# Weight sums for the FFN moved to later steps, a gate split cut in two, and combination factors moved to GpSimd

## The chip, the cores and the metric

The kernel runs on one core of a Trainium2 chip. The metric is the device time of one execution in microseconds (us). A core has five engines that run side by side, each in its own program order: TensorE (PE, matrix products; its weight loads show as PEld), VectorE (DVE), ScalarE (ACT), GpSimd (POOL) and SyncE (SP), which here only issues DMA transfers. Engines wait for one another through semaphores. SBUF is the memory that the engines work in, PSUM the one that PE writes into.

## The reference

One transformer layer on 1024 tokens of width 1024, in float32:

```
h    = rms_norm(x, g1) * (1 + sc1) + sh1
proj = h @ w_in                     # qa ka va | qb kb vb | gates
o_a  = neighbourhood_attention(qa, ka, va, rpb)       # 8 heads
o_g, lse_g = dilated_window_attention(qb, kb, vb, g)  # 3 groups of 4 heads
wts  = softmax(stack(lse_g), axis=0)                  # over the 3 groups
o_b  = sum_g wts[g] * o_g
gate_a, gate_b = sigmoid(gates + b_gate)
x    = x + gt1 * ((gate_a * (o_a @ w_a) + gate_b * (o_b @ w_b)) @ w_o)
h2   = rms_norm(x, g2) * (1 + sc2) + sh2
a, up = split(h2 @ w_ffn_in)                          # FFN
x    = x + gt2 * ((silu(a) * up) @ w_ffn_out)
```

`wts`, the weights over the three dilated groups, are the combination factors of this case.

## The kernel before

Every large product is made of float32 pieces that PE takes at a faster rate: a float32 tile of weights is split into a high part `whi` (ACT, L129 or L1204) and the rest `wlo`, the difference (GpSimd or DVE, L132 or L1210), and the product is the sum of three passes, whi by hi, wlo by hi and whi by lo. A second layer of economy forms products of 2 x 2 blocks from fewer block products, for which sums and differences of weight blocks are needed beforehand. For the gates these are made by `gate_prep`: the blocks w11 and w12 are only split, and x1 and x4 come from sums (L868, L870, L875) that are then split (L132). For the first two column sets of the FFN they are made by `w1_combos`: four loads of 256 KB (L953, tile `w1m`), four sums of 128 by 512 on GpSimd (L957, L959, L961, L963) and four stores (L965) into a scratch tensor in device memory, which the FFN reads back at the far end of the kernel, from 867 us of the trace on.

The middle of the kernel is one loop over steps n = 6 to 91. A step holds some chunks of projection products (from the stream of input projections up to step 75, L1248; from step 76 the gate products, L880), and around them the attention pieces of one or two heads: score products (L579), maximum and bias and exponentials (DVE L593, ACT L594 and L597, the reciprocals L596), turns of probabilities and of queries and keys through PE (L605 and L477), and their copies back (DVE L609, L505, L506; ACT L503, L504, L611). `qk` is the tile of turned queries and keys that the score products read; its high part is written by ACT and by DVE L505, its rest by ACT L504 and DVE L506. DVE also evicts the products (L397, L446, L1168 to L1171) and normalizes queries and keys (L406, L415, L416, L426). L505, L506, L397, L446 and L593 read a PSUM operand; L415, L416 and L426 read two operands that both lie in SBUF.

PE's order is written out by hand and is the same row for row in both kernels. On the other engines and on the SP queue a list scheduler places the instructions, by priorities that follow the order in which the code issues them and by its own costs, except that those under `pin` keep their place among one another. So where the code issues something decides what comes ahead of what on DVE, ACT, GpSimd and SP. Waits are set by data: an instruction that stands ready behind one that waits has to wait too.

Three tables and a function say at which step the pieces here are issued. `GPREP` (L31) maps a step to a pair of gate columns and a part of `gate_prep`: part -2 loads w11 and w12 of a pair, 0 splits them, -1 loads the other two blocks, and 1 makes x1 and x4. `GLOAD` (L32) loads later pairs whole (tile `gl`, two transfers of 1 MB, L841). `W1MIX` (L33) gives the first of the five steps over which each of the two calls of `w1_combos` is spread (L1368). `combine_stats` (L728) works out the combination factors in five parts in steps 68 to 72 from the loaded statistics `sa`, on arrays of 128 by 32: minimum (L738, L739), differences (L742), exponentials (ACT, L743), sum of weighted terms (L745 to L750), reciprocal (L751) and final factors (L754). The factors `fe` are read from step 80 on.

In the trace, steps 68 to 75 lie at about 420 to 485 us, 80 to 91 at about 503 to 588 us.

Of the kernel before, what the change touches and what calls it, by code (L numbers as in the profile page):

```python
# [27 lines left out]
MORD = (3, 4, 5, 6, 7, 2, 0, 1)  # L28
GPAIRS, GGROUPS = ((5, 6), (7, 2), (0, 1), (3, 4)), ((3, 4, 5), (6, 7, 2), (0, 1))
GPHASE = ("w11", "w12", "x1", "x4")  # L30
GPREP = {72: (0, -2), 73: (0, 0), 74: (0, -1), 76: (0, 1), 82: (1, 0), 84: (1, 1), 86: (2, 0), 88: (2, 1), 90: (3, 0)}  # L31
GLOAD = {81: 1, 85: 2, 89: 3}  # L32
W1MIX = (69, 74)  # L33
MC11 = {0: (5, 6, 7, 2), 1: (0, 1)}
MKEEP = {3: 3, 4: 4, 5: 5, 6: 6, 7: 7}
MSLOT = {4: 2, 5: 0, 6: 1}
# [12 lines left out]
def hybrid_layer(ctx: ExitStack, tc: tile.TileContext, x, colp, wada1, wada2, bada2, wqkv, wg, wpa, wpb,  # L49
                 wo, w1, w2, hgain, ropeg, rope, rbias, bmask, g2r, out):  # L50
    nc = tc.nc
# [676 lines left out]
    def combine_stats(part):  # L728
        nm = [cb["sa"][:, :, g, :, 0:2] for g in range(3)]
        sm = [cb["sa"][:, :, g, :, 2:4] for g in range(3)]  # L730
        if part == 0:
            cb["nM"] = ap_.tile([128, 8, 2, 2], F32, tag="nM", bufs=1, name="nM")
            cb["fe"] = ap_.tile([128, 3, 8, 2, 2], F32, tag="fe", bufs=1, name="fe")
            cb["tw"] = ap_.tile([128, 8, 2, 2], F32, tag="tw", bufs=1, name="tw")
            cb["tot"] = ap_.tile([128, 8, 2, 2], F32, tag="tot", bufs=1, name="tot")
        nM, fe, tw, tot = (cb[z] for z in ("nM", "fe", "tw", "tot"))
        if part == 0:
            nc.vector.tensor_tensor(nM, nm[0], nm[1], op=ALU.min)  # L738
            nc.vector.tensor_tensor(nM, nM, nm[2], op=ALU.min)  # L739
        elif part == 1:  # L740
            for g in range(3):
                nc.vector.tensor_sub(fe[:, g], nM, nm[g])  # L742
            nc.scalar.activation(fe, fe, AF.Exp)  # L743
        elif part == 2:
            nc.vector.tensor_mul(tot, fe[:, 0], sm[0])  # L745
            nc.vector.tensor_mul(tw, fe[:, 1], sm[1])
            nc.vector.tensor_add(tot, tot, tw)
        elif part == 3:
            nc.vector.tensor_mul(tw, fe[:, 2], sm[2])
            nc.vector.tensor_add(tot, tot, tw)  # L750
            nc.vector.reciprocal(tot, tot)  # L751
        else:
            for g in range(3):
                nc.vector.tensor_mul(fe[:, g], fe[:, g], tot)  # L754

    def combine_prep(i):
        pr, g, hf = i // 6, (i % 6) // 2, i % 2
# [87 lines left out]
    def gate_prep(p, part):  # L845
        pr = GPAIRS[p]
        if part == -2:
            for i in pr:
                for q in (0, 1):
                    graw[i, q] = gate_raw(i, q)  # L850
            return
        if part == 0:
            for nm, q in (("w11", 0), ("w12", 1)):
                for i in pr:
                    gwt[i, nm] = wsplit(graw[i, q])
            return
        if part == -1:
            z = big("wgx")
            for i in pr:
                for q in (2, 3):  # L860
                    graw[i, q] = gate_raw(i, q) if i == pr[0] else z[:, 512 * q - 1024:512 * q - 512]
            for q in (2, 3):
                pin(nc.sync.dma_start(graw[pr[1], q], wg[pr[1], :, 4 * q:4 * q + 4, :]))
            return
        eng = nc.vector if p == 3 else nc.gpsimd
        for i in pr:
            r = [graw.pop((i, q)) for q in range(4)]
            eng.tensor_add(r[2], r[2], r[3])  # L868
            gwt[i, "x1"] = wsplit(r[2])
            eng.tensor_sub(r[2], r[2], r[0])  # L870
            if p < 3:
                nc.sync.dma_start(sig_d[i, 4], r[2])
            else:
                glate[i] = r[2], r[3]
            eng.tensor_sub(r[1], r[1], r[2])  # L875
            gwt[i, "x4"] = wsplit(r[1], eng)
# [1159 lines left out]
```

## Time and profile before

| | us |
|---|---|
| runs shown | 1478.35, 1470.94, 1472.72 |
| median of these | 1472.72 |
| profiled execution | 1472.6 |
| its span (first to last instruction) | 1470.8 |
| PE busy in the span | 1449.9 |
| DVE busy | 1102.8 |
| GpSimd busy | 732.5 |
| ACT busy | 703.9 |

The profiled execution's own time is 1.8 us above its span, and 0.1 us under the median of the runs. Engine times are the sum of their busy stretches; several engines are busy at once, so they add up to more than the span. The mean granted TensorE clock is 0.998 of full speed: it stands at 1.00 nearly throughout. In a timeline, a row gives the start, the time, the engine, the line, the operation, what is written from what, and in brackets the idle time before it and what ended it.

### The profile page before, as it was taken

To read this page: it belongs to the slowest core of one execution; us is meant where nothing else is said; L and a number is where in the kernel's file an instruction comes from. 1 tells how busy PE (TensorE), PEld (TensorE's weight loads), DVE (VectorE), ACT (ScalarE), POOL (GpSimd) and SP (SyncE) were. 2 spreads that over 40 slices of the span, in tenths; PEclk is the share of its full clock that TensorE was granted. 3 is DMA by queue.
4 is the path that set the end of the run, shared out by engine and by line. 5 is a ranking of instruction groups with operands and counts; after the bars stand their busy time and mean duration, and the time that the engine had idled before them with its cause. 6 is when DMAs were issued, how large, how long until landed. Compare 5 with 4: busy or idle time off the path is not lost.

```text
span 1470.8 us, 24489 instructions
## 1 busy us (share of the span) xinstructions
PE 1449.9 (99%) x8024; PEld 1235.4 (84%) x8024; DVE 1102.8 (75%) x2120; ACT 703.9 (48%) x1771; POOL 732.5 (50%) x706
## 2 busy tenths in 40 slices
PE   8999999999999999999999999999999999999998
PEld 7999999999888777888878888888888888888886
DVE  6688867858688765795877696888777777599578
ACT  5566665666777764554432453332232223354442
POOL 0353466655544455355522303777677775104464
PEclk9999999999999999999999999999999999999999
DMA  9658686766758676955374334445433334898353
GB/s 359 221 169 261 186 266 194 231 198 211 231 176 264 220 243 209 367 191 173 122 257 146 100 101 164 132 148 179 164 100 106 105 107 151 287 348 302 109 157 101
DMA packets 191568, 285.18 MB, mean 194 GB/s; under 512 B 29744, under 2 KB 91856, under 8 KB 190672
## 3 DMA queue, kind: packets, MB, share of 16 engines
q1 hardware_dynamic: 172864, 269.96, 55.4%
q10 hardware_dynamic: 18576, 13.64, 2.8%
q8 instruction: 64, 1.05, 0.3%
q14 instruction: 64, 0.52, 0.1%
HBM read 218.67 MB, written 64.86 MB: 193 GB/s over the span
## 4 chain that ended last, share of the span: by engine, by line
PE 48%; DVE 3%; ACT 1%; DMA 1%; issue 0%; POOL 0%; SPq 0%; ACTq 0%; DVEq 0%
PE ps_s L1695 8%; PE ps_d L1695 7%; PE ps_v L1695 7%; PE ps_t L1695 6%; PE ps_s L1871 4%; PE ps_d L1871 4%; PE ps_t L1871 3%; PE ps_v L1871 3%; PE ps_s L1630 2%; PE ps_d L1630 2%; PE ps_v L1630 1%; DVE sg L1485 1%; DVE wlo L132 1%; DMA sg<-sig_d 1%; ACT h2T L1486 1%; DVE sg L1484 0%
## 5 line engine op out<-in xcount | busy, mean ns | idle before, releaser
L129 ACT ACTIVATE whi<-raw 128x512 fp32r<-128x512 f32 (+2 forms) x265 | 158.3, 608 | 180.0 <-PE ps_s L1871 34.9
L132 POOL TENSOR_TENSOR wlo<-raw,whi 128x512 fp32r<-128x512 f32 (+2 forms) x94 | 128.5, 1375 | 117.3 <-ACT whi L129 114.3
L132 DVE TENSOR_TENSOR wlo<-raw,whi 128x512 fp32r<-128x512 f32 (+1 forms) x171 | 148.9, 888 | 50.1 <-ACT whi L129 47.0
L379 PE MATMUL ps_d<-whi,hT 128*128 128x384 f32 x384 | 101.3, 338 | 0.0
L1645 POOL TENSOR_TENSOR e<-e,c 128x512 f32<-128x512 f32 x44 | 68.8, 1565 | 60.9 <-DVE c L1775 36.8
L129 ACT ACTIVATE whi<-ws 128x512 fp32r<-128x512 f32 x60 | 37.6, 627 | 118.6 <-DVE ws L1712 80.9
L1248 PE MATMUL ps_d<-whi,hT 128*128 128x384 f32 x312 | 88.1, 342 | 1.3 <-DVE hT L1169 1.1
L880 PE MATMUL ps_d<-hT,whi 128*128 128x512 f32 x264 | 84.2, 400 | 0.0
L132 POOL TENSOR_TENSOR wlo<-m,whi 128x512 fp32r<-128x512 f32 x35 | 51.0, 1463 | 51.5 <-ACT whi L129 51.5
L1643 ACT ACTIVATE e<-e 128x512 f32<-128x512 f32 x44 | 27.5, 630 | 98.4 <-DVE e L1778 69.7
L379 PEld LDWEIGHTS ps_d<-whi,hT 128*128 128x128 f32 x384 | 69.6, 188 | 0.6 <-issue 0.6
L1248 PE MATMUL ps_d<-whi,smix 128*128 128x384 f32 x240 | 68.1, 343 | 0.9 <-DMA smix<-t_d 0.6
L1210 POOL TENSOR_TENSOR wlo<-raw,whi 128x384 fp32r<-128x384 f32 x48 | 49.8, 1054 | 30.6 <-ACT whi L1204 30.5
L379 PE MATMUL ps_d<-wlo,hT 128*128 128x384 f32 x192 | 64.2, 334 | 0.0
L658 ACT ACTIVATE P<-P,st 128x256 f32<-128x256 f32 (+2 forms) x100 | 45.6, 458 | 36.2 <-DVE st L656 36.2
L1210 POOL TENSOR_TENSOR wlo<-chain,whi 128x384 fp32r<-128x384 f32 x36 | 37.5, 1055 | 51.0 <-ACT whi L1204 51.0
L1695 PE MATMUL ps_v<-h2T,whi 128*128 128x512 f32 x192 | 59.2, 389 | 0.0
L1695 PE MATMUL ps_s<-h2T,whi 128*128 128x512 f32 x192 | 59.1, 389 | 0.0
L1248 PEld LDWEIGHTS ps_d<-whi,hT 128*128 128x128 f32 x312 | 57.0, 188 | 2.4 <-DVE hT L1169 1.4
L132 POOL TENSOR_TENSOR wlo<-gl,whi 128x512 fp32r<-128x512 f32 x30 | 41.1, 1384 | 32.4 <-ACT whi L129 32.2
L1644 DVE TENSOR_TENSOR e<-e 128x512 f32<-128x512 f32 x44 | 43.6, 999 | 17.7 <-ACT e L1643 17.4
L1695 PE MATMUL ps_d<-h2T,whi 128*128 128x512 f32 x184 | 56.7, 390 | 0.0
(485 smaller groups left out, 4647.8 us busy)
## 6 DMA issues: line engine op xcount, KB each, us to landing
raw<-in_w_dram SPq DMA_DIRECT2D x139, 256.0 KB, 3.3
raw<-in_wqkv_dram SPq DMA_DIRECT2D x116, 192.0 KB, 3.7
ga_d<-e SPq DMA_DIRECT2D x77, 256.0 KB, 2.3
raw<-ga_d SPq DMA_DIRECT2D x77, 256.0 KB, 2.6
smix<-t_d SPq DMA_DIRECT2D x72, 256.0 KB, 4.0
m<-in_w_dram SPq DMA_DIRECT2D x44, 256.0 KB, 5.3
xt<-in_x_dram SPq DMA_DIRECT2D x16, 512.0 KB, 6.4
land<-in_wada_dram SPq DMA_DIRECT2D x16, 512.0 KB, 9.5
```

What stands on the lines that cost most here:

```text
L129: h = nc.scalar.activation(hi[:, :n], r, AF.Copy)
L132: (eng or nc.gpsimd).tensor_sub(lo[:, :n], r, fview(hi[:, :n]))
L379: nc.tensor.matmul(pd[:, :384], tok(a, k, t), U.w[k][b][:, :384], start=(k == 0 and i == 0), stop=(k == KT - 1 and i == 2))
L658: nc.scalar.activation(C.P[h][:nq, c], C.P[h][:nq, c], AF.Exp, scale=-1.0, bias=nm, accum_out=sm)
L880: nc.tensor.matmul(pb, w[x][:, k * 128:(k + 1) * 128], b[y][k], start=(k == 0 and q == 0), stop=(k == 3 and q == 2))
L1210: nc.gpsimd.tensor_sub(lo[:, :384], z, fview(hi[:, :384]))
L1248: nc.tensor.matmul(pd[:, :384], lhs, w[k][b][:, :384], start=(k == 0 and i == 0), stop=(k == 3 and i == 2))
L1630: nc.tensor.matmul(pbs[hf], h2T[a][:, k, t * 128:(t + 1) * 128], wow[hf, k][b], start=(n == 0 and (a, b) == PASS[0]), stop=(n == KT - 1 an ...
L1644: nc.vector.tensor_mul(sg, sg, a)
L1645: nc.gpsimd.tensor_mul(sg, sg, up)
L1695: nc.tensor.matmul(pb, w[p][:, k * 128:(k + 1) * 128], b[q][:, k], start=(k == 0 and i == 0), stop=(k == 3 and i == 2))
L1871: nc.tensor.matmul(pb[m], o[0][a][:, m * 128:(m + 1) * 128], o[1][b], start=(k == 0 and i == 0), stop=(k == HT - 1 and i == 2))
```

## The change

`W1MIX` moves the two sets of FFN weight sums from steps 69 to 73 and 74 to 78 to steps 80 to 84 and 85 to 89. `GPREP` splits w11 of both columns of the first pair in step 73 (part 5) and w12 in step 75 (part 6), instead of both in step 73. In `combine_stats` the eleven differences, products and sums go from DVE to GpSimd; the two minima and the reciprocal stay on DVE, the exponential on ACT.

```diff
@@ -28,9 +28,9 @@
 MORD = (3, 4, 5, 6, 7, 2, 0, 1)
 GPAIRS, GGROUPS = ((5, 6), (7, 2), (0, 1), (3, 4)), ((3, 4, 5), (6, 7, 2), (0, 1))
 GPHASE = ("w11", "w12", "x1", "x4")
-GPREP = {72: (0, -2), 73: (0, 0), 74: (0, -1), 76: (0, 1), 82: (1, 0), 84: (1, 1), 86: (2, 0), 88: (2, 1), 90: (3, 0)}
+GPREP = {72: (0, -2), 73: (0, 5), 74: (0, -1), 75: (0, 6), 76: (0, 1), 82: (1, 0), 84: (1, 1), 86: (2, 0), 88: (2, 1), 90: (3, 0)}
 GLOAD = {81: 1, 85: 2, 89: 3}
-W1MIX = (69, 74)
+W1MIX = (80, 85)
 MC11 = {0: (5, 6, 7, 2), 1: (0, 1)}
 MKEEP = {3: 3, 4: 4, 5: 5, 6: 6, 7: 7}
 MSLOT = {4: 2, 5: 0, 6: 1}
@@ -739,19 +739,19 @@
             nc.vector.tensor_tensor(nM, nM, nm[2], op=ALU.min)
         elif part == 1:
             for g in range(3):
-                nc.vector.tensor_sub(fe[:, g], nM, nm[g])
+                nc.gpsimd.tensor_sub(fe[:, g], nM, nm[g])
             nc.scalar.activation(fe, fe, AF.Exp)
         elif part == 2:
-            nc.vector.tensor_mul(tot, fe[:, 0], sm[0])
-            nc.vector.tensor_mul(tw, fe[:, 1], sm[1])
-            nc.vector.tensor_add(tot, tot, tw)
+            nc.gpsimd.tensor_mul(tot, fe[:, 0], sm[0])
+            nc.gpsimd.tensor_mul(tw, fe[:, 1], sm[1])
+            nc.gpsimd.tensor_add(tot, tot, tw)
         elif part == 3:
-            nc.vector.tensor_mul(tw, fe[:, 2], sm[2])
-            nc.vector.tensor_add(tot, tot, tw)
+            nc.gpsimd.tensor_mul(tw, fe[:, 2], sm[2])
+            nc.gpsimd.tensor_add(tot, tot, tw)
             nc.vector.reciprocal(tot, tot)
         else:
             for g in range(3):
-                nc.vector.tensor_mul(fe[:, g], fe[:, g], tot)
+                nc.gpsimd.tensor_mul(fe[:, g], fe[:, g], tot)
 
     def combine_prep(i):
         pr, g, hf = i // 6, (i % 6) // 2, i % 2
@@ -849,8 +849,8 @@
                 for q in (0, 1):
                     graw[i, q] = gate_raw(i, q)
             return
-        if part == 0:
-            for nm, q in (("w11", 0), ("w12", 1)):
+        if part in (0, 5, 6):
+            for nm, q in (("w11", 0), ("w12", 1))[part // 6:2 - part % 6 // 5]:
                 for i in pr:
                     gwt[i, nm] = wsplit(graw[i, q])
             return
```

With the scheduler placing DVE, ACT, GpSimd and SP, the tables move more than they name. DVE in steps 71 and 72, before: `qk` is the turned-query tile, `qn` the normalized queries and keys, `rz` their factors.

```order
L446 TENSOR_TENSOR hT<-hT,ps_d 128x128
L415 SCALAR_TENSOR_TENSOR rz<-ss_7312,ry 128x8
L416 SCALAR_TENSOR_TENSOR rz<-rz,rv 128x8
L505 SCALAR_TENSOR_TENSOR qk<-ps_v,hg,qk 128x2x64
L426 SCALAR_TENSOR_TENSOR qn<-qn,rz 128x256 x2
L506 TENSOR_TENSOR qk<-ps_v,qk 128x2x64
L397 TENSOR_TENSOR qn<-hT,ps_d 128x256
L446 TENSOR_TENSOR hT<-hT,ps_d 128x128
L406 TENSOR_REDUCE ss_7482<-sq 128x4
L593 ISA P,sx<-ps_s,rb 128x256
L593 ISA sx 128x1
```

The same place on DVE in the changed kernel:

```order
L397 TENSOR_TENSOR qn<-hT,ps_d 128x256
L446 TENSOR_TENSOR hT<-hT,ps_d 128x128
L505 SCALAR_TENSOR_TENSOR qk<-ps_v,hg,qk 128x2x64
L506 TENSOR_TENSOR qk<-ps_v,qk 128x2x64
L397 TENSOR_TENSOR qn<-hT,ps_d 128x256
L415 SCALAR_TENSOR_TENSOR rz<-ss_7304,ry 128x8
L446 TENSOR_TENSOR hT<-hT,ps_d 128x128
L416 SCALAR_TENSOR_TENSOR rz<-rz,rv 128x8
L426 SCALAR_TENSOR_TENSOR qn<-qn,rz 128x256 x2
L406 TENSOR_REDUCE ss_7473<-sq 128x4
L593 ISA P,sx<-ps_s,rb 128x256
```

Before, the two L426 stand between L505 and L506; now L505 and L506 follow each other and stand ahead of L415, L416 and L426.

GpSimd in steps 70 to 76, before (-) and now (+): the splits of `raw` 128x384 are the stream's, the four of 128x512 are those of w11 and w12, and `w1m` are the FFN weight sums.

```order
-L957 TENSOR_TENSOR w1m<-w1m 128x512
-L1210 TENSOR_TENSOR wlo<-raw,whi 128x384 x2
-L959 TENSOR_TENSOR w1m<-w1m 128x512
-L1210 TENSOR_TENSOR wlo<-raw,whi 128x384 x2
-L961 TENSOR_TENSOR w1m<-w1m 128x512
-L963 TENSOR_TENSOR w1m<-w1m 128x512
+L1210 TENSOR_TENSOR wlo<-raw,whi 128x384 x4
 L132 TENSOR_TENSOR wlo<-raw,whi 128x512 x4
-L957 TENSOR_TENSOR w1m<-w1m 128x512
-L959 TENSOR_TENSOR w1m<-w1m 128x512
 L868 TENSOR_TENSOR raw<-raw 128x512
 L868 TENSOR_TENSOR wgx<-wgx 128x512
```

The six sums that lay there are gone; the four splits still follow one another without anything between them, and the first sums of x1 (L868) stand directly behind them.

GpSimd in steps 80 to 86, where the first L957 now stands just ahead of this piece: `gl` are the whole columns of the second pair of gates.

```order
+L959 TENSOR_TENSOR w1m<-w1m 128x512
+L868 TENSOR_TENSOR gl<-gl 128x512
+L132 TENSOR_TENSOR wlo<-gl,whi 128x512
+L868 TENSOR_TENSOR gl<-gl 128x512
+L132 TENSOR_TENSOR wlo<-gl,whi 128x512 x3
 L961 TENSOR_TENSOR w1m<-w1m 128x512
+L132 TENSOR_TENSOR wlo<-gl,whi 128x512
 L963 TENSOR_TENSOR w1m<-w1m 128x512
-L868 TENSOR_TENSOR gl<-gl 128x512
-L132 TENSOR_TENSOR wlo<-gl,whi 128x512
-L868 TENSOR_TENSOR gl<-gl 128x512
-L132 TENSOR_TENSOR wlo<-gl,whi 128x512 x4
```

Two sums stand ahead of the pair's first L868, and two among its splits. On the SP queue, the first set's loads (L953) moved to a place ahead of the first two `gl` loads (L841), the second set's loads ahead of the next two and its stores (L965) ahead of the last two; the loads of the first pair's other two blocks (L120 and L863), which stood behind four stores and four loads of `w1m`, now stand without them. On GpSimd the factors stand among the stream's splits and sums L1199 of steps 68 to 70.

## Rows read from the trace of the kernel before

**Rows 1.** Page, part 1: engine, busy us, share of the span, instructions.
```profile
PE 1449.9 (99%) x8024; PEld 1235.4 (84%) x8024; DVE 1102.8 (75%) x2120; ACT 703.9 (48%) x1771; POOL 732.5 (50%) x706
```

**Rows 2.** Waits of the PE, whole span: line, waited for, total us, times, longest.
```profile
PE ps_s L579 <- DVE qk L506: 3.0, 1, 3.0
...
PE ps_d L1248 <- DVE hT L1169: 1.1, 1, 1.1
...
PE ps_v L477 <- DVE sx L596: 0.6, 1, 0.6
```

**Rows 3.** Windows: us, busy PE, PEld, DVE, ACT, POOL, PEclk, DMA share, GB/s.
```profile
420.00:440.00 20.00, 18.95 (x137) 16.62 (x136) 17.46 (x58) 15.05 (x47) 9.03 (x9) 1.00 0.49 148
467.50:470.60 3.10, 0.09 (x2) 0.00 (x0) 3.10 (x6) 1.49 (x4) 2.16 (x2) 1.00 1.07 393
470.60:474.00 3.40, 3.38 (x22) 2.83 (x23) 2.01 (x8) 2.02 (x8) 0.00 (x0) 0.50 1.03 341
510.00:514.00 4.00, 4.00 (x24) 3.27 (x24) 2.12 (x6) 3.19 (x11) 0.00 (x0) 1.00 0.62 194
514.00:520.00 6.00, 6.00 (x46) 4.48 (x46) 4.22 (x12) 2.96 (x9) 1.26 (x2) 1.00 0.97 360
```

**Rows 4.** Timeline of DVE, 463 to 475: start, us, line, operation, [idle before].
```profile
463.12 0.41 DVE L593 CUSTOM_DVE_ANT_0 P<-ps_s,rb 128x256 f32<-128x256 f32 x1
...
467.26 1.20 DVE L416 SCALAR_TENSOR_TENSOR rz<-rz,rv 128x8 f32<-128x8 f32 x1
468.38 0.42 DVE L505 SCALAR_TENSOR_TENSOR qk<-ps_v,hg,qk 128x128 fp32r<-128x128 f32 x1
468.72 1.56 DVE L426 SCALAR_TENSOR_TENSOR qn<-qn,rz 128x256 f32<-128x256 f32 x2
470.20 0.36 DVE L506 TENSOR_TENSOR qk<-ps_v,qk 128x128 fp32r<-128x128 f32 x1
```

**Rows 5.** Timeline of ACT, 465 to 475.
```profile
466.62 0.43 ACT L504 ACTIVATE qk<-ps_v 128x128 fp32r<-128x128 f32 x1
```

**Rows 6.** Timeline of PE, 454 to 486.
```profile
461.06 0.62 PE L579 MATMUL ps_s<-qk 64*128 64x256 f32 x6
...
467.20 0.38 PE L579 MATMUL ps_s<-qk 64*128 64x256 f32 x2
470.62 0.80 PE L579 MATMUL ps_s<-qk 64*128 64x256 f32 x4 [3.03 <-DVE qk L506]
```

**Rows 7.** Timeline of GpSimd (POOL), 444 to 500.
```profile
465.91 3.75 POOL L132 TENSOR_TENSOR wlo<-raw,whi 128x512 fp32r<-128x512 f32 x3 [0.47 <-ACT whi L129]
...
478.20 1.28 POOL L868 TENSOR_TENSOR raw<-raw 128x512 f32<-128x512 f32 x1
```

**Rows 8.** Timeline of SP's queue, 459 to 480.
```profile
467.92 3.16 SPq L953 DMA_DIRECT2D w1m<-in_w_dram  x4
471.44 1.16 SPq L120 DMA_DIRECT2D raw<-in_wg_dram  x2
```

**Rows 9.** Timeline of DVE, 474 to 486.
```profile
478.69 2.52 DVE L426 SCALAR_TENSOR_TENSOR qn<-qn,rz 128x256 f32<-128x256 f32 x2
```

**Rows 10.** Timeline of DVE, 418 to 432.
```profile
424.89 1.04 DVE L746 TENSOR_TENSOR tw<-fe,sa 128x32 f32<-128x32 f32 x1
```

**Rows 11.** Groups of GpSimd by line, 100 to 300: busy us, mean ns.
```profile
L434 POOL TENSOR_TENSOR rb<-qn,rtab 128x32 f32<-128x32 f32 x35 | 12.2, 348 | 0.0
```

**Rows 12.** Timeline of GpSimd, 498 to 560.
```profile
518.74 1.29 POOL L868 TENSOR_TENSOR gl<-gl 128x512 f32<-128x512 f32 x1 [19.71 <-DMA gl<-in_wg_dram]
519.99 1.32 POOL L132 TENSOR_TENSOR wlo<-gl,whi 128x512 fp32r<-128x512 f32 x1
...
547.31 1.29 POOL L132 TENSOR_TENSOR wlo<-gl,whi 128x512 fp32r<-128x512 f32 x1
```

**Rows 13.** Timeline of PE, 518 to 530.
```profile
523.37 0.40 PE L880 MATMUL ps_d<-hT,wlo 128*128 128x512 f32 x1
```

**Rows 14.** Timeline of PE, 554 to 560.
```profile
556.35 0.40 PE L880 MATMUL ps_d<-hT,wlo 128*128 128x512 f32 x1
```

## The prediction

> **What bounds the kernel now.** I read the engines' busy times first: PE is busy 99% of the span, the next engine, DVE, 75% [rows 1]. So time can only come from PE: from its waits, from its clock, or from new waits put on it. The list of PE's waits, read next, puts a single one on top: score products L579 wait 3.0 us for DVE L506, the last writer of the turned queries and keys; below it, among the waits between 400 and 500 us, are 1.1 us for L1169 and 0.6 us for L596 [rows 2]. The windows then show what the long one costs beyond itself: in 467.5 to 470.6 PE is busy 0.09 of 3.10 us, and in the 3.40 us behind it the granted clock is 0.50, the lower of its two levels (1.2 instead of 2.4 GHz), while PE is busy 3.38 us [rows 3]. At full clock that work takes 1.7 us, so the dip costs 1.7 and stall and dip together 4.7 us.
>
> Last, the timelines around the stall, which tell why L506 is late. ACT's part of the same tile is there at 467.05 (466.62 + 0.43) [rows 5], and PE reaches its first row of L579 at 467.20 [rows 6]. But on DVE, L505 starts at 468.38 behind an L416 that took 1.20 us for 128 by 8 elements, and the two L426, 1.56 us together, stand between L505 and L506 [rows 4]. In the same stretch GpSimd runs three of the first gate's four low-part splits without a break, 465.91 to 469.66, 1.25 us each [rows 7]: L416 ends at 468.46, where the second of them ends (468.41). At 478.69, where GpSimd runs an L868 [rows 7], two L426 take 2.52 us [rows 9]. So operations of DVE that read two SBUF operands get in only where a GpSimd instruction ends, while L505 and L506, which read PSUM, run in 0.42 and 0.36 us in the midst of the splits. The Trainium skill, "SBUF — State Buffer", section on who interferes with whom, has the same: a DVE instruction with two SBUF inputs and a GpSimd one that reads SBUF exclude each other for a whole instruction, one with at most one SBUF input is free; the trace agrees (1.20 us against 0.36 to 0.42).
>
> **The change part by part.** All sums are on the profiled execution: 1472.6 us, 1.8 above its span and 0.1 below the median shown.
>
> *The stall at 467 us.* The stall goes by order, not by a faster engine. In the changed DVE order L505 and L506 follow each other ahead of L415, L416 and L426. ACT's part ends at 467.05, L505 and L506 take 0.42 and 0.36 [rows 4, 5], so L506 ends by about 467.7, and PE, at its first L579 rows until 467.58 [rows 6], waits 0.1 us or nothing: −3.0. The clock fell in this stretch only right behind the stall; with the stall I take away the dip: −1.7. Bounds: 0, if something else on DVE holds L505 as long, and −4.7.
>
> *The two-step gate split.* The four low-part splits still stand back to back on GpSimd, and their loads and ACT's high parts are issued where they were. I give this part 0 by itself (0 to −0.4, L506's remaining lateness).
>
> *What is late next.* Two things follow the splits more closely now. The loads of the first pair's other blocks went out at 471.44, behind the second set's L953 at 467.92 [rows 8] and four stores; without these they go out at 467.9 at the latest, and earlier by the stores' time, right behind the step's own loads. And the two L957 and L959 that stood ahead of L868 are gone. So x1's sums, which began at 478.20 [rows 7], can begin where the splits end, 469.66, and GpSimd works without gaps from 465.9 to about 472.2 (five instructions of 1.25). DVE's L415, L416 and two L426, from 467.9 on, then get in one at each end of a GpSimd instruction: 468.4, 469.7, 470.9, 472.2. Queued behind them on DVE is L593, which begins the softmax of the scores just made. Undisturbed it comes 2.06 us behind the first L579 (463.12 against 461.06) [rows 4, 6], here at 469.3; held, at 472.2. For the probabilities' turn the next step leaves about 2 us of that. The same early sums meet the short last step of the stream, where the chain has no slack already: PE waits 0.6 us for L596 there [rows 2]. Bounds: 0, if the held operations fit into the step, and +4.7, another stall like the first with its dip. Nearest is the 0.6 us wait, twice, with a little from the longer hold: I take +1.4.
>
> *Combination factors.* Eleven instructions of 128 by 32 leave DVE in the stretch 420 to 440, where it is busy 17.46 of 20 us [rows 3]; one of them is L746, held for 1.04 us [rows 10]. Ahead of L1169, for which PE waits 1.1 us, stand only the three L742. Bounds: 0 and −1.1; I take −0.4, for those three and the smaller hold of what follows. On GpSimd the nearest operation of that shape, L434, takes 348 ns [rows 11]: 11 × 0.35 = 3.8 us, laid into 10.97 us of idle time (9.03 of 20 busy) [rows 3]. The last three wait for DVE's reciprocal, and the stream's splits are queued behind them on GpSimd; the factors are read only from step 80 on. If the cover were gone, 3.8 us of GpSimd would delay splits, and PE with them: that is in the upper end.
>
> *Weight sums in steps 80 to 89.* Eight sums of 1.3 us, eight loads and eight stores, 2 MB in and 2 MB out, all moved. Their result is read from 867 us on, so only what they delay counts. First set: L957 and L959 fit into the 19.71 us in which GpSimd sat idle until `gl` landed [rows 12]. Their 1 MB of loads stands ahead of the `gl` loads on the SP queue: at 360 GB/s, the rate when nothing else limits [rows 3], 2.9 us. In the stretch where they can go out, 510 to 514, a DMA share of 0.62 leaves 0.38 × 4 = 1.5 us of room [rows 3], so `gl` lands about 1.4 us later. The first low part from it ends at 521.31 and PE wants it at 523.37 [rows 12, 13]: 2.06 us of slack. That hides it; but ACT, which makes the high parts of `gl` in its own order between softmax pieces, may pass some of it on. I take +0.3 (0 to +2.9). Second set: two sums of the first set among the splits free `gl`'s buffer 2.6 us later, and 1 MB of loads adds 2.9: 5.5 us, against 556.35 − 548.60 = 7.75 us of slack in the next pair [rows 12, 14]. At 0, with +4.7 (a stall with its dip) if the cover is gone; the last pair has a similar distance.
>
> Sum: −3.0 −1.7 +1.4 −0.4 +0.3 = −3.4, so 1472.6 − 3.4 = 1469.2 us.
>
> **The rivals.**
> *B, the wait moves on by a step.* x1's sums hold L415, L416 and L426 as worked out above, L593 comes at 472.2, and PE, instead of waiting for `qk` at 467, waits about 3 us for the probabilities at about 472 or in the short step, and the clock falls again. For it: the two L426 of 2.52 us at 478.69 beside only two L868. Against it: the normalized queries that L426 makes are not needed until steps later, and only the order on DVE passes the hold on. The sum has +4.7 in place of +1.4: 1472.5 us. The rule of the Trainium skill ("SBUF — State Buffer", who interferes with whom) that the second one blocks in full for the whole instruction speaks for this end.
>
> *C, slower: `gl` comes late.* The weight sums push each of the three later pairs' `gl` past the slack: decided by whether the first low part slips by more than 2.06 us (second pair) and 7.75 us (third), where I reckon 1.4 and 5.5. Each pair then costs a stall with a dip, 4.7 us: 1472.6 − 3.0 − 1.7 − 0.4 + 14.1 + 1.4 = 1483.0. For it: the DMA share is 0.97 in 514 to 520 already [rows 3], so anything added there is late in full. Against it: both slacks.
>
> *D, the change does not do what it says.* Splitting in two steps leaves the splits together, and DVE is still held by them ahead of L505: the order ahead of it has the evictions L397 and L446 alone, but if L505 slips behind a wait of those, stall and dip stay: 1472.6 − 0.4 + 0.3 = 1472.5.
>
> **How the numbers follow.** My forecast 0.60, with 1466.2 to 1471.5 as its own range: the low end is 1472.6 less all that rows 2 and 3 offer between 400 and 500 us, 3.0 + 1.7 + 1.1 + 0.6 = 6.4. B 0.20 (1471.5 to 1474), D 0.08, C 0.12, of which a third with a single late pair (1473 to 1476) and two thirds with two or three. Half a per cent, about what a measurement of this kernel can tell, is 7.4 us: faster means below 1465.4, slower above 1480.1. Faster then needs more than the waits that I can name, by a shift of the runs against the profiled execution or by a wait elsewhere: 0.09. Slower is most of C: 0.08. The rest, 0.83, is within. The range, 1465.5 to 1476.5, takes in the forecast, B and D and a single late pair.
>
> **What would show it.** Right: no wait of L579 for L506 near 467 us, L505 and L506 next to each other, and a granted clock of 1.00 throughout 460 to 480; L868 starting near 470; some wait of 0.5 to 1.5 us of L605 or L477 for ACT or DVE in 470 to 485; no factor on DVE and less than 1.1 us at L1169; `gl` landing 1 to 2 us later with no wait of L880. Wrong: a wait over 2 us with a clock of 0.50 behind it anywhere in 420 to 590. If it stands in 470 to 485 it is B, at 467 D, at L880 or behind a low part of `gl` C.

## The result and the profile after

| | us |
|---|---|
| before, median of 6 runs | 1472.22 |
| after, median of 6 runs | 1484.41 (1483.52 to 1484.92) |
| ratio after / before | 1.0083, 95% interval 1.0071 to 1.0096 |
| profiled execution, and its span | 1484.92, 1483.1 |

The change made the kernel 0.83% slower; the predicted 1469.2 us and the range up to 1476.5 both miss it. PE has the same instructions in the same order in both kernels, so the time can be followed matmul by matmul: the start of one in the trace of after, less its start in the trace of before.

| stretch in before, us | shift at its start and end, us | lost (+) or gained (−) |
|---|---|---|
| 0 to 460 | 0, −1.7 | −1.7 |
| 460 to 475, the stall at 467 | −1.7, −6.6 | −4.9 |
| 475 to 490 | −6.6, −3.3 | +3.3 |
| 490 to 545 | −3.3, −2.9 | +0.4 |
| 545 to 562, third pair of gates | −2.9, 4.6 | +7.5 |
| 650 to 690 | 4.6, 7.1 | +2.5 |
| 735 to 765, the merge of the gates | 7.1, 12.5 | +5.4 |
| 765 to the end | 12.5, 12.3 | −0.2 |

The first row is not the change's: it arises at about 30 us, long before any edited instruction, and every kernel below shows something like it (0.4 to 2.7 us less at 100 us), though the code there is the same.

The page of after, part 1, against [rows 1]: PE's busy time grew by 5.7 us of the 12.3, by work at the lower clock; the rest is waits.

```profile
PE 1455.6 (98%) x8024; PEld 1237.9 (83%) x8024; DVE 1096.1 (74%) x2109; ACT 703.9 (47%) x1771; POOL 733.3 (49%) x717
```

The waits of PE in after between 380 and 800 us (line, waited for, total, times, longest). L506 of [rows 2] is gone; of the two on top the first is new, and the second has grown: before, it read `PE ps_d L1630 <- DVE sg L1484: 1.3, 1, 1.3`.

```profile
PE ps_d L880 <- ACT P L597: 4.9, 1, 4.9
PE ps_d L1630 <- DVE sg L1484: 4.0, 1, 4.0
PE ps_v L620 <- DVE PT L609: 1.5, 1, 1.5
PE ps_s L880 <- DVE wlo L132: 1.1, 1, 1.1
PE ps_t L352 <- DVE acc L367: 1.0, 1, 1.0
...
PE ps_d L1248 <- DVE hT L1169: 0.6, 1, 0.6
```

The windows of after (us, busy PE, PEld, DVE, ACT, POOL, clock, DMA share, GB/s). Behind each of the three new waits the clock is low. What that costs is the busy time by the missing share of the clock: 4.38 × 0.34 = 1.5, 5.05 × 0.45 = 2.3 and 5.00 × 0.50 = 2.5 us. With the waits, 1.5, 4.9 and 4.0 − 1.3, this makes 3.0, 7.2 and 5.2 us, against the shifts of 3.3, 7.5 and 5.4.

```profile
460.00:477.00 17.00, 15.50 (x119) 12.99 (x117) 13.71 (x43) 12.62 (x43) 11.73 (x9) 1.00 0.57 184
...
477.00:482.00 5.00, 4.38 (x20) 3.61 (x21) 3.85 (x15) 4.97 (x16) 3.58 (x3) 0.66 0.09 26
...
555.80:563.00 7.20, 5.05 (x12) 3.80 (x12) 4.25 (x7) 2.59 (x8) 7.20 (x7) 0.55 0.37 125
...
752.00:757.00 5.00, 5.00 (x12) 3.93 (x13) 4.12 (x5) 1.79 (x4) 2.53 (x2) 0.50 0.82 246
```

**467 us: the stall is gone.** DVE in after, 463 to 478, the answer to [rows 4] and [rows 9]:

```profile
463.88 0.45 DVE L505 SCALAR_TENSOR_TENSOR qk<-ps_v,hg,qk 128x128 fp32r<-128x128 f32 x1 [0.84 <-ACT qk L504]
464.24 0.40 DVE L506 TENSOR_TENSOR qk<-ps_v,qk 128x128 fp32r<-128x128 f32 x1
...
465.51 1.12 DVE L416 SCALAR_TENSOR_TENSOR rz<-rz,rv 128x8 f32<-128x8 f32 x1
466.66 0.76 DVE L426 SCALAR_TENSOR_TENSOR qn<-qn,rz 128x256 f32<-128x256 f32 x2
...
473.74 0.98 DVE L416 SCALAR_TENSOR_TENSOR rz<-rz,rv 128x8 f32<-128x8 f32 x1
474.75 1.83 DVE L426 SCALAR_TENSOR_TENSOR qn<-qn,rz 128x256 f32<-128x256 f32 x2
...
476.57 0.40 DVE L609 COPY PT<-ps_t 128x256 f32<-128x256 f32 x1
```

L506 ends at 464.64, and the score products L579 begin without a wait at 465.44. L416 still takes 1.12 us beside GpSimd's splits, but it now stands behind L506. The clock is 1.00 in 460 to 477.

**477 us: part of it is given back.** GpSimd, 462 to 477, the answer to [rows 7]:

```profile
462.81 3.80 POOL L132 TENSOR_TENSOR wlo<-raw,whi 128x512 fp32r<-128x512 f32 x3 [0.48 <-ACT whi L129]
467.99 1.30 POOL L868 TENSOR_TENSOR raw<-raw 128x512 f32<-128x512 f32 x1 [1.38 <-DMA raw<-in_wg_dram]
470.79 1.28 POOL L868 TENSOR_TENSOR wgx<-wgx 128x512 f32<-128x512 f32 x1 [1.50 <-DMA wgx<-in_wg_dram]
...
473.39 1.30 POOL L870 TENSOR_TENSOR raw<-raw 128x512 f32<-128x512 f32 x1
474.77 1.52 POOL L875 TENSOR_TENSOR raw<-raw 128x512 f32<-128x512 f32 x1
```

L868 moved from 478.20 to 467.99, and the sums L870 and L875 now run beside the next L416 and L426 of DVE, which take 0.98 and 1.83 us. The copy L609 of the turned probabilities stands behind them and starts at 476.57. The Trainium skill, "SBUF — State Buffer", section on who interferes with whom, has it that such DVE operations with two SBUF inputs contend with a GpSimd instruction that reads SBUF, while those with one or none, outside the two-port modes, do not. The trace agrees: 0.98 and 1.83 us here, against 0.76 for the two L426 at 466.66, where GpSimd had just ended its splits (466.61); L505 and L506, with a PSUM operand, take 0.45 and 0.40 beside the splits.

**553 us and 751 us: two new stalls.** PE's timeline in after, at both places:

```profile
557.95 1.19 PE L880 MATMUL ps_d<-hT,whi 128*128 128x512 f32 x2 [4.86 <-ACT P L597]
...
751.85 4.21 PE L1630 MATMUL ps_d<-wr,h2T 128*128 128x512 f32 x9 [3.99 <-DVE sg L1484]
```

The wait of 4.86 us is put down to ACT L597, but the product of L880 reads no probabilities. It needs weights (the high part from ACT L129, the low part from GpSimd or DVE L132) and a PSUM bank that DVE L888 has emptied. The high part was there at 551.54 (below) and GpSimd's low part at 553.53 (552.25 + 1.28), about when PE would have wanted it (556.35 [rows 14] less the 2.9 us by which PE is ahead: 553.4), so the bank was late. ACT's timeline, 550 to 557, with what stands behind the next high parts:

```profile
550.91 0.63 ACT L129 ACTIVATE whi<-gl 128x512 fp32r<-128x512 f32 x1 [4.76 <-DMA gl<-in_wg_dram]
553.46 2.19 ACT L129 ACTIVATE whi<-gl 128x512 fp32r<-128x512 f32 x4 [1.92 <-DMA gl<-in_wg_dram]
555.56 0.60 ACT L594 ACTIVATE P<-P,sx 128x384 f32<-128x384 f32 x1
```

The same place on ACT before:

```profile
545.86 0.63 ACT L129 ACTIVATE whi<-gl 128x512 fp32r<-128x512 f32 x1
...
550.22 2.19 ACT L129 ACTIVATE whi<-gl 128x512 fp32r<-128x512 f32 x4 [2.27 <-DMA gl<-in_wg_dram]
```

And DVE, 548 to 559:

```profile
556.28 0.17 DVE L596 RECIPROCAL sx<-sx 128x1 f32<-128x1 f32 x1 [5.78 <-ACT P L594]
...
557.12 1.28 DVE L888 TENSOR_TENSOR gc<-gc,ps_d 128x512 f32<-128x512 f32 x2
```

The same place on DVE before:

```profile
550.56 0.69 DVE L888 TENSOR_TENSOR gc<-gc,ps_d 128x512 f32<-128x512 f32 x1 [1.61 <-PE ps_d L880]
551.27 0.56 DVE L593 CUSTOM_DVE_ANT_0 P<-ps_s,rb 128x384 f32<-128x384 f32 x1
...
553.04 0.17 DVE L596 RECIPROCAL sx<-sx 128x1 f32<-128x1 f32 x1 [0.73 <-ACT P L594]
```

So the chain runs: `gl` lands late (the first high part at 550.91 in place of 545.86, the next four at 553.46 in place of 550.22); ACT, in order, has the exponentials L594 behind them; DVE's L596 waits 5.78 us for L594; and L888, which before stood ahead of the softmax, now stands behind L596. The bank comes free with the first L888, one of the two of 1.28 us that begin at 557.12, and PE starts at 557.95. The releaser that the view names ended at about the same time.

Why did L888 move? In the program text of after, the tile `gc` that it writes takes over one of the pool's eight large buffers from `oacc`, which first has to be stored (SP L1376); before, it takes one that had long been free. `w1m` of the second set occupies two of these buffers in steps 85 to 89, which shifts the turns of all that follow, and the scheduler, as I read it, puts an instruction with a late input further back; that the buffer moves L888, E10 and E13 below show.

SP's queue in after shows both transfers, 538 to 547, and the fourth pair's, 573 to 580:

```profile
538.87 1.92 SPq L953 DMA_DIRECT2D w1m<-in_w_dram  x4
540.92 0.83 SPq L841 DMA_DIRECT2D gl<-in_wg_dram  x2
...
546.58 0.62 SPq L1376 DMA_DIRECT2D o_d<-oacc  x1
...
573.20 4.50 SPq L915 DMA_DIRECT2D sig_d<-gc  x2
577.75 1.94 SPq L965 DMA_DIRECT2D w_d<-w1m  x4
579.78 0.99 SPq L841 DMA_DIRECT2D gl<-in_wg_dram  x2
```

The fourth pair's loads on SP before, then their first use on ACT, before and after:

```profile
573.18 0.88 SPq L841 DMA_DIRECT2D gl<-in_wg_dram  x2
```

```profile
578.12 0.63 ACT L129 ACTIVATE whi<-gl 128x512 fp32r<-128x512 f32 x1 [1.31 <-DMA gl<-in_wg_dram]
```

```profile
586.38 0.63 ACT L129 ACTIVATE whi<-gl 128x512 fp32r<-128x512 f32 x1 [1.77 <-DMA gl<-in_wg_dram]
```

For the fourth pair the four stores L965 stand between L915 and the loads: `gl` is issued 6.6 us later than before (573.18), while PE is only 4.6 us late there, and its first use by ACT comes at 586.38 in place of 578.12, 8.3 us later. The Trainium skill, "Perfetto Trace Analysis", section on the DMA instruction of the HWDGE kind, says that the bar of such an instruction doesn't contain the movement of the data. The trace agrees: bars of 0.99 us, and 6.6 us until the data are used. From there the lateness goes through the splits and sums of the merge on ACT, DVE and GpSimd, which have little slack: the last L1484 before L1630 starts at 751.12 in place of 741.39, 9.7 us later, where PE is 7.1 us later. On DVE the merge runs about 7.5 us later than before from 589 to 611 us (of before), and about 10 us later from 633 on; in between, the scheduler's order on ACT, DVE and GpSimd is not that of before (see E9 and E12). The 2.5 us in 650 to 690 are, but for 0.4, the two waits of 1.1 and 1.0 us for L132 and L367; the clock is 1.00 there.

### The profile page after: what moved, and what is told of

The parts are those of the page before. It is cut to its first block, busy times and chain, and to the rows that moved or that the text cites. A ratio compares the mean times of both kernels' runs of the same rounds, so it can differ in the third digit from the quotient of the medians.

```text
span 1483.1 us, 24495 instructions
## 1 busy us (share of the span) xinstructions
PE 1455.6 (98%) x8024; PEld 1237.9 (83%) x8024; DVE 1096.1 (74%) x2109; ACT 703.9 (47%) x1771; POOL 733.3 (49%) x717
## 4 chain that ended last, share of the span: by engine, by line
PE 48%; DVE 3%; ACT 1%; DMA 1%; issue 0%; POOL 0%; SPq 0%; ACTq 0%; DVEq 0%; POOLq 0%
PE ps_s L1695 8%; PE ps_d L1695 7%; PE ps_v L1695 7%; PE ps_t L1695 6%; PE ps_s L1871 4%; PE ps_d L1871 4%; PE ps_t L1871 3%; PE ps_v L1871 3%; PE ps_d L1630 2%; PE ps_s L1630 2%; PE ps_v L1630 1%; DVE sg L1485 1%; DVE wlo L132 1%; PE ps_t L1617 0%; ACT h2T L1486 0%; DVE sg L1484 0%
## 5 line engine op out<-in xcount | busy, mean ns | idle before, releaser
L129 ACT ACTIVATE whi<-raw 128x512 fp32r<-128x512 f32 (+2 forms) x265 | 158.1, 608 | 189.6 <-PE ps_s L1871 39.8
L132 POOL TENSOR_TENSOR wlo<-raw,whi 128x512 fp32r<-128x512 f32 (+2 forms) x94 | 129.1, 1382 | 116.1 <-ACT whi L129 104.7
L132 DVE TENSOR_TENSOR wlo<-raw,whi 128x512 fp32r<-128x512 f32 (+1 forms) x171 | 146.5, 874 | 48.5 <-ACT whi L129 46.5
L129 ACT ACTIVATE whi<-ws 128x512 fp32r<-128x512 f32 x60 | 37.7, 628 | 119.1 <-DVE ws L1712 71.8
L880 PE MATMUL ps_d<-hT,whi 128*128 128x512 f32 x264 | 86.5, 410 | 4.9 <-ACT P L597 4.9
L132 POOL TENSOR_TENSOR wlo<-m,whi 128x512 fp32r<-128x512 f32 x35 | 51.2, 1471 | 50.7 <-ACT whi L129 49.6
L132 POOL TENSOR_TENSOR wlo<-gl,whi 128x512 fp32r<-128x512 f32 x30 | 39.1, 1316 | 44.2 <-ACT whi L129 40.3
L880 PEld LDWEIGHTS ps_d<-hT,whi 128*128 128x128 f32 x264 | 49.0, 194 | 14.3 <-ACT P L597 5.1
```

What stands on the lines that cost most here:

```text
L129: h = nc.scalar.activation(hi[:, :n], r, AF.Copy)
L132: (eng or nc.gpsimd).tensor_sub(lo[:, :n], r, fview(hi[:, :n]))
L880: nc.tensor.matmul(pb, w[x][:, k * 128:(k + 1) * 128], b[y][k], start=(k == 0 and q == 0), stop=(k == 3 and q == 2))
```

## The experiments

The theories: the loss comes from the weight sums in their new place, by (a) the loads and stores on SP's queue ahead of `gl`, (b) the sums on GpSimd ahead of the splits, or (c) the buffers that the second set takes. "Shift" is as in the table above; "third pair" is its change from 545 to 562, "late chain" that from 650 to 765. All ratios are to runs of before on the same chip, with 95% intervals.

### Which part of the change

**E1.** After, with the sums back where they were:

```diff
-W1MIX = (80, 85)
+W1MIX = (69, 74)
```

> The change without its first part: the FFN weight sums are back in steps 69 to 78, the two-step gate split and the factors on GpSimd stay. T1 (loads and stores of the weight sums, put ahead of the gl transfers on the SP queue, make gl land late) and T2 (the eight sums on GpSimd among the gl splits make the splits late) both put the loss on this part: no waits of 4 to 5 us at about 553 and 750 us, 1470 to 1474 us. DVE's order has L426 between L505 and L506 again, so the stall of 3 us at 467 us should be back. T3 (the loss comes from the other two parts): still 1482 to 1486 us.

Measured: 1475.24 us, ratio 1.0018 (1.0009 to 1.0028). No loss at the third pair and none in the late chain; L579 waits 3.0 us for L506 again, and L1169 costs 2.0.

**E2.** Before, with the sums moved and nothing else:

```diff
-W1MIX = (69, 74)
+W1MIX = (80, 85)
```

> The kernel before with the weight sums alone moved to steps 80 to 89. T1 and T2: gl of the third pair late, a wait of L880 at about 553 to 557 us with a clock drop, and a late chain at about 745 us: 1482 to 1488 us. L426 stands between L505 and L506 here, so the stall at 467 us should stay as well unless the splits come at another time. T3: 1470 to 1474 us.

Measured: 1482.58 us, 1.0065 (1.0051 to 1.0079). Third pair +4.9, late chain +7.5; L579 still waits 1.4 us, with L426 between L505 and L506.

What follows: the two late places, 15.4 us together in after, come with the move of the sums and go without it. E1 is still 0.18% above before, with its two waits. The stall at 467 needs both, the move and the factors off DVE: with one alone 1.4 or 3.0 us of it stay.

**E14.** After, without the two-step split:

```diff
-GPREP = {72: (0, -2), 73: (0, 5), 74: (0, -1), 75: (0, 6), 76: (0, 1), ...
+GPREP = {72: (0, -2), 73: (0, 0), 74: (0, -1), 76: (0, 1), ...
```

> The change without its second part: both w11 and w12 split in step 73 again. By the order on GpSimd and ACT, which is the same, and on DVE, nearly the same, the two-step split does nothing: 1483 to 1486 us, with the same three places of loss. If the split in two steps matters, the stall at 467 us comes back or the wait at 477 us changes: 2 us or more either way.

Measured: 1482.05 us, 1.0065 (1.0052 to 1.0078). The same gain at 467 (−4.9), the same loss at 477 (+3.9) and the same two late places. The wait at 553 is 3.1 us in place of 4.9; the kernels do not differ there in code, and E2 and E12 have 3.0 and 3.2. The traces tell these waits apart by how late `gl` is against PE: on the time of before (the start less PE's shift at 545) ACT begins the four high parts at 554.6 to 554.7 in E2, E12 and E14, which lose 4.9 to 5.0 us at the third pair, and at 556.4 in after, which loses 7.5. In after the loads go out 0.7 to 0.8 us later against PE; why the data come another 1.0 us later is not known. The intervals of E14 and of after just meet, so a small cost of the split is not excluded.

### Queue, sums or buffers

**E5.** In every step the loads of `gl` are issued ahead of the weight sums:

```diff
-        for j in range(2):
-            if 0 <= n - W1MIX[j] < 5:
-                w1_combos(j, n - W1MIX[j])
         if n in GPREP:
             gate_prep(*GPREP[n])
         if n in GLOAD:
             gate_load(GLOAD[n])
+        for j in range(2):
+            if 0 <= n - W1MIX[j] < 5:
+                w1_combos(j, n - W1MIX[j])
```

> The change with one thing turned round: where a step has both, the gl transfers are issued ahead of the weight sums' part, so that on the SP queue the second set's loads stand behind the gl loads of the third pair, and its stores behind those of the fourth. The sums stay on GpSimd among the splits. T1: gl lands at about 546 and 550 us as before, no wait of L880 there, the fourth pair's gl on time too: 1468 to 1473 us. T2: 1480 us or more.

Measured: 1476.18 us, 1.0027 (1.0017 to 1.0037). The late chain is gone (+0.2). At the third pair +8.1 stays, with `gl` nearly on time (high parts at 546.31 and 550.07). Here the view's releaser is L888 (`PE ps_d L880 <- DVE gc L888: 4.7, 1, 4.7`); DVE and SP in E5:

```profile
557.65 1.28 DVE L888 TENSOR_TENSOR gc<-gc,ps_d 128x512 f32<-128x512 f32 x2 [1.92 <-DMA o_d<-oacc]
```

```profile
543.52 3.11 SPq L953 DMA_DIRECT2D w1m<-in_w_dram  x3
...
552.41 0.32 SPq L1376 DMA_DIRECT2D o_d<-oacc  x1
```

L888 waits for the store of `oacc`, the old owner of its buffer, which was issued 5.8 us later than in after: three loads of `w1m` now go out at 543.52, and the queue then stood for 3.4 us at the load behind them, L763. So theory (a), read as `gl` alone, falls for the third pair: what was taken off one transfer fell on the other.

**E6.** After, with the eight sums on GpSimd left out (the stores then write the loaded blocks):

```diff
-            pin(nc.gpsimd.tensor_add(r[3], r[2], r[3]))
+            pass
```

(and so for the other three)

> The change without the eight sums on GpSimd (the loads and stores of the weight sums stay, so the FFN reads wrong weights for two column sets). T1: gl of the third pair still lands 3 to 5 us late, L880 waits 4 to 5 us near 553 us: the larger part of the loss stays, 1478 us or more; the fourth pair may be better, since its stores no longer wait for a sum. T2: 1468 to 1473 us.

Measured: 1477.21 us, 1.0035 (1.0022 to 1.0049). Third pair +1.2, late chain +8.0. The sums' 1.3 us each are not what makes the chain late. For the third pair it leaves (b) and (c) side by side, since without the sums the buffers of `w1m` have fewer users; E13 and E10 part them. On the time of before its four high parts begin at 552.6, 3.8 us earlier than in after, with L888 behind L596 as there.

**E9.** The second set two steps later:

```diff
-W1MIX = (80, 85)
+W1MIX = (80, 87)
```

> The change with the second set of weight sums two steps later (steps 87 to 91 instead of 85 to 89). Then its loads stand behind the gl loads of the third pair, its stores behind those of the fourth, and gc of the third pair gets a buffer that the first set left long before, not that of oacc. T1 (queue: w1m transfers ahead of gl) and T4 (buffers: the sums hold two of the eight large buffers, so gc inherits the buffer of oacc, whose store is late, and its eviction L888 moves behind L596 on DVE) both expect the wait of L880 at 553 us and the late chain at 747 us to go: 1468 to 1473 us.

Measured: 1472.20 us, 1.0004 (0.9993 to 1.0014). No loss at the third pair, and `gl` of the fourth is on time (its high part at 574.44, 3.7 us earlier than before, as PE is). Yet L1630 waits 3.6 us and the late chain is +5.1. One sum now stands between the fourth pair's splits on GpSimd (first E9, then the next split in before):

```profile
582.16 1.30 POOL L963 TENSOR_TENSOR w1m<-w1m 128x512 f32<-128x512 f32 x1
...
587.59 1.29 POOL L132 TENSOR_TENSOR wlo<-gl,whi 128x512 fp32r<-128x512 f32 x1 [2.87 <-ACT whi L129]
```

```profile
590.98 1.29 POOL L132 TENSOR_TENSOR wlo<-gl,whi 128x512 fp32r<-128x512 f32 x1 [3.85 <-ACT whi L129]
```

But the sum is not what makes the chain late: the split behind it is 3.4 us earlier than before, as PE is 3.7, and DVE stays 3.4 us earlier to 611. The lateness comes up between 631 and 675 us of before, and behind it DVE is only 0.9 us earlier. In this stretch the scheduler's order on ACT, DVE and GpSimd is not that of before. So late loads of the fourth pair's `gl` are not the only way into the late chain. The changed order of the merge is likely to be the other one, but no run tests it by itself.

**E10 and E11.** Only the first set moved (E11), and the same with two large buffers held from step 85 to 89 by tiles that carry no data (E10):

```diff
-W1MIX = (80, 85)
+W1MIX = (80, 74)
```

```diff
+        if n == 85:
+            hold = big("hold"), big("hold")
+        if n in (85, 89):
+            for z in hold:
+                pin(nc.gpsimd.memset(z[:, :1], 0.0))
```

> The same as the run that holds two buffers, without the two buffers: second set in steps 74 to 78, first in 80 to 84. T1 and T4: no wait of L880 at 553 us, no late chain at 747 us; the stall at 467 us stays away (L505 and L506 stand together): 1467 to 1473 us. If the first set alone, loaded ahead of the second pair's gl, costs something, it shows as a wait of L880 or L605 at 518 to 530 us.

> The change with the second set in steps 74 to 78 as before, so no traffic and no sums of it in steps 85 to 89, but with two large buffers allocated at step 85 and touched there and at step 89 (memsets of one column), so that gc of the third pair again gets the buffer of oacc. T4: L880 waits 2 to 5 us near 553 us with a clock drop behind it, 1474 to 1480 us, though gl lands as before. T1: no such wait, 1468 to 1473 us. Both: no late chain at 747 us beyond the 1.3 us of before.

Measured: E11 1470.72 us, 0.9989 (0.9979 to 0.9998); E10 1470.12, 0.9989 (0.9979 to 1.0). Behind 490 us each loses 0.9 us in all, 0.4 (E10) and 0.7 (E11) of it by 545, and at most 0.4 at either late place. In E10 L880 waits 0.2 us for L888. So the first set's move costs at most 0.7 us, and the buffers alone at most 0.4, as long as no large transfer is ahead.

### One link at a time

**E12.** `gl` ahead of the sums in step 89 alone (the fourth pair):

```diff
+        if n == 89:
+            gate_load(GLOAD[n])
         for j in range(2):
             if 0 <= n - W1MIX[j] < 5:
                 w1_combos(j, n - W1MIX[j])
 ...
-        if n in GLOAD:
+        if n in GLOAD and n != 89:
             gate_load(GLOAD[n])
```

> The change with the fourth pair's gl loads issued ahead of the second set's last part in step 89 alone: its four stores stand behind these loads on the SP queue, all else as in the change. T1 for the fourth pair: the loss of 2.5 us at 666 to 676 us and of 5.3 us at 742 to 757 us goes, the wait of L880 at 553 us stays: 1475 to 1479 us. If the late chain is only what the wait at 553 us left behind, it stays at 1482 to 1486 us.

Measured: 1475.57 us, 1.0023 (1.0013 to 1.0032). Third pair +5.0 as expected of an untouched place; the late chain is gone (−0.4). SP and PE in E12 (L1632 is L1630 of the other kernels):

```profile
569.78 4.51 SPq L915 DMA_DIRECT2D sig_d<-gc  x2
574.38 0.89 SPq L841 DMA_DIRECT2D gl<-in_wg_dram  x2
575.32 2.10 SPq L965 DMA_DIRECT2D w_d<-w1m  x4
```

```profile
742.93 2.34 PE L1632 MATMUL ps_d<-wr,h2T 128*128 128x512 f32 x9 [0.95 <-DVE sg L1486]
```

The order of these two in the code, 2.0 us of issue and 1 MB of stores ahead of the loads, is worth 8.3 us behind 650 (+7.9 against −0.4). L915's 4.5 us are in both kernels, so they are not the difference. But the edit changes more than the queue: from 575 to 680 us (of before) the scheduler's order on ACT, DVE and GpSimd is that of before in E12, row for row, and another in after. All kernels here divide in the same way: E1, E5, E10, E11, E12, E16 and E17 have the order of before and a late chain of −0.4 to +1.2; after, E2, E6, E9, E13 and E14 have another and lose 5.1 to 8.2. So E12 does not part the late loads from the order that comes with them, and no run does.

**E13.** After, with half of the second set in other tiles, so that `gc` no longer follows `oacc`:

```diff
-            w1c[n] = [z[:, 512 * q:512 * q + 512] for z in (big("w1m"), big("w1m")) for q in range(2)]
+            w1c[n] = [z[:, 512 * q:512 * q + 512] for z in (big("w1m"),) + (() if n else (big("w1m"),)) for q in range(2)]
+            if n:
+                w1c[n] += [wp.tile([128, 512], F32, tag="raw", bufs=NRAW, name="w1m") for _ in range(2)]
```

> The change with half of the second set's tiles taken from the small raw buffers in place of a large one: transfers, sums and their order on the SP queue stay, but gc of the third pair no longer gets oacc's buffer, and its eviction L888 stands ahead of L593 and L596 on DVE again. T5 (both links are needed: late gl holds ACT's softmax pieces, and L888 stands behind them only because of the buffer): the wait of L880 near 553 us falls under 1.5 us, most of the 7.6 us lost there is back, the late chain at 747 us stays: 1476 to 1480 us. T1 alone (late gl is enough): the wait stays at 3 us or more, 1481 us or more.

Measured: 1478.96 us, 1.0043 (1.003 to 1.0056). Third pair 0, late chain +8.2, and 0.9 more from 562 to 650. ACT and DVE in E13:

```profile
552.66 2.19 ACT L129 ACTIVATE whi<-gl 128x512 fp32r<-128x512 f32 x4 [1.89 <-DMA gl<-in_wg_dram]
```

```profile
548.09 0.69 DVE L888 TENSOR_TENSOR gc<-gc,ps_d 128x512 f32<-128x512 f32 x1 [1.50 <-PE ps_d L880]
```

`gl` is late here too: on the time of before the four high parts begin at 555.1, between after (556.4) and E2, E12 and E14 (554.6 to 554.7), which lose 4.9 us or more. But L888 runs ahead of the softmax again, and PE waits for nothing. With E10 and E5 this settles the third pair: a late transfer (`gl`, or in E5 the store of `oacc`) and an L888 that a changed buffer has put behind it. Either alone costs 0 (E13) to 0.4 us (E10), both together 1.2 (E6, `gl` the least late) to 8.1 (E5), and 7.5 in after.

**E17.** E13 and E12 together.

> The change with both repairs at once: half of the second set's tiles in the small raw buffers, so that gc of the third pair does not get oacc's buffer, and the fourth pair's gl loads ahead of the second set's last part in step 89. All transfers and sums stay in steps 80 to 89. If buffer and queue are the whole loss: no wait of L880 near 553 us, the waits at 666 to 676 us and the long one at 747 us gone, 1469 to 1473 us. If the sums or the traffic as such cost something more: 1475 us or above.

Measured: 1471.52 us, 1.0001 (0.999 to 1.0013). No wait at 553 or at 666 to 676; L1630's product waits 2.5 us, and the late chain is +1.2. The two edits take back the loss, to within what these runs can tell; with them the order of the merge is that of before as well.

**E16.** E11 with the factors back on DVE:

```diff
-                nc.gpsimd.tensor_sub(fe[:, g], nM, nm[g])
+                nc.vector.tensor_sub(fe[:, g], nM, nm[g])
```

(and so in the other six lines of the change in `combine_stats`)

> First set of weight sums in steps 80 to 84, second in 74 to 78, two-step gate split, factors back on DVE: the run with the two sets so placed, without the third part of the change. On DVE the two L426 stand between L505 and L506 again. If the factors' place is what moved L505 and L506 together and that is what ended the stall: a wait of 1.4 to 3 us of L579 for L506 near 467 us comes back, 1472 to 1475 us. If the earlier or later sums alone end it: 1469 to 1472 us.

Measured: 1470.65 us, 0.999 (0.998 to 1.0), the same as E11. Its PE waits 1.6 us at 467, with the clock at 0.57 from 468 to 472; DVE in E16:

```profile
464.77 0.44 DVE L505 SCALAR_TENSOR_TENSOR qk<-ps_v,hg,qk 128x128 fp32r<-128x128 f32 x1
465.13 1.82 DVE L426 SCALAR_TENSOR_TENSOR qn<-qn,rz 128x256 f32<-128x256 f32 x2
466.87 0.38 DVE L506 TENSOR_TENSOR qk<-ps_v,qk 128x128 fp32r<-128x128 f32 x1
```

E11 gains 4.9 at 467 and gives 3.3 back by 490; E16 gains 1.6 there and another 0.8 by 490. So 1.6 and 2.4 us remain. Once the first set is moved, the factors on GpSimd buy nothing that these runs can tell: they take the stall from one step to the next.

## Why the prediction was wrong, step by step

*The stall at 467 us* (−3.0 −1.7): right, in place, cause and size (−4.9). What the working did not say is that two parts of the change are needed for the new order; E1, E2 and E16 show it.

*The two-step gate split* (0): right as far as the places go that it touches (E14).

*What is late next* (+1.4): the mechanism was right (L416 and L426 held by the gate's sums, the turn of the probabilities late), the size was not: +3.3, a wait of 1.5 us and a clock of 0.66 in 477 to 482. I had GpSimd work without gaps from 469.7 on. In fact L868 waited 1.38 and 1.50 us for its loads, and L870 and L875 fell on the next step's L416 and L426 instead. Between kernels with this code the size varies from 1.6 to 4.0 us.

*Combination factors* (−0.4): L1169 waits 0.6 in place of 1.1 us. But E1, with the same factors and the sums in their old place, has 2.0, and E2 and E16, with the factors on DVE and sums moved away, have 0.2 and 0.4. So the moved sums shortened the wait, not the factors: the number was near by luck, and the reason given for it was wrong.

*Weight sums, first set* (+0.3): right in size; 490 to 545 lost 0.4 us, and 0.7 in E11, where this set alone moved.

*Weight sums, second set* ("At 0, with +4.7 (a stall with its dip) if the cover is gone; the last pair has a similar distance"): this is the step that failed. It was worth +7.5 at the third pair and +7.9 in the late chain. Three things were wrong with it.
- The slack of 7.75 us was read on one path, from a split on GpSimd to the product that uses it. That path just held: the low part was ready at 553.53, when PE would have wanted it. But its slack was gone: against PE the low part slipped by 7.8 us (4.9 by the clock of the trace, 2.9 because PE was earlier), where I had 5.5. The lateness that PE waited for took another path, through ACT's order (high parts ahead of L594) and DVE's order (L596 ahead of L888) to the PSUM bank. A transfer's slack is the shortest over every instruction queued behind its users.
- Buffers were counted as a delay of `gl` alone. That two more large tiles change whose buffer `gc` follows, and with it the order on DVE, was not looked at, though the program of the changed kernel showed both. E10 and E13 together show that the loss needs it.
- "A similar distance" for the last pair was not worked out. On SP's queue the stores of the second set stand directly ahead of its loads, 2.0 us of issue, and the merge behind it has little slack: L1630 waited 1.35 us already before. Nor was the scheduler's order of the merge, which the move changed, compared with that of before.

Beside that, the time saved at 467 to 490 works against the slack: loads that are issued at the same time as before (540.92) meet a PE that is 2.9 us earlier.

*Rivals.* C was the right kind, decided by `gl` past its slack, and with three pairs at 4.7 us it gave 1483.0 us against 1484.41. It was two places at 7.5 and 7.9 instead, and the low part that it named is not what PE waited for, so that the total came so near is luck. I gave it 0.12 on the strength of "both slacks", which were the wrong ones. B did happen in part (+3.3), D did not.

The working took 2.9 us for a megabyte, at 360 GB/s; [rows 3] also have 393, which makes 2.7 us and changes nothing in it.

What stays open: how the late chain is shared between late loads and the scheduler's order of the merge (E12 changes both; E9 has the order without late loads and loses 5.1 us; E6 shows that without the sums on GpSimd it stays), and why the start of the kernel differs by up to 2.7 us from trace to trace.

## What to carry to other kernels

When work that uses a shared pool and a shared queue is moved, list for every tile behind it whose buffer it now follows and what that one still waits for, and for every queue what now stands ahead of the next load; and compare the order on every engine for as long behind the change as the scheduler may have altered it. Take a transfer's slack over all that stands in order behind its users on their engines, not on the path to the next product alone. And where PE is the bound, a saved stall has to be charged against all slacks behind it: of the 4.9 us gained here 3.3 were given back within 15 us, and the best version found (E11, 0.9979 to 0.9998) is 0.1% faster than before, as is E16 without the factors' move.

## What the runs showed that I had not expected

- After a wait of 2.54 us (E17) L1630's nine products take 2.35 us, at a clock of 1.00; after one of 3.58 (E9) or 3.99 (after) they take 4.21, in after at 0.50. So 1 us more of waiting costs nearly 2 us more of work at the lower clock. The length of the wait alone does not tell: behind the 1.50 us at 477 in after the clock is 0.66.
- GpSimd runs the factors' 128 by 32 operations in 0.25 to 0.26 us, less than the 0.35 that I had taken from L434 [rows 11], and a quarter of the 1.04 that DVE needed for L746 when it was held [rows 10]; not held, DVE took 0.18 (L742 in before).
- The view's releaser can be a coincidence: in after the 4.86 us are put down to ACT L597, in E5 the same wait to DVE L888, and of the two only L888 touches the bank that the product writes.
